# Reordering the first projection and the modulation loads of a one-core transformer block

## The chip, the cores and the metric

The kernel runs on one core of one Trainium2 chip, as one program. The metric is the device time of an execution in microseconds, from three executions of the kernel before. The profile is one further execution, taken by the hardware profiler.

Engines are named as the profile names them: PE (TensorE), PEld (its weight loads), DVE (VectorE), ACT (ScalarE), POOL (GpSimd), SP (SyncE, which issues the DMAs).

## The reference, cut to what matters

Two blocks are computed for 512 positions of 1024 channels. Only the first lines of the first block matter here:

```
mod = silu(c) @ w_ada + b_ada                  # 6 x 1024 numbers, from one vector c
shift1, scale1, gate1, shift2, scale2, gate2 = split(mod)
h = rms_norm(x, norm1_w) * (1 + scale1) + shift1
proj = h @ w_in                                # split into dn_q, dn_k, dn_v, ..., gates
q, k, v = silu(causal_dwconv(dn_q, dn_k, dn_v))
o_a = gated_delta_rule(l2_norm(q), l2_norm(k), v, g, beta)   # recurrence over 8 chunks of 64
o_a = rms_norm(o_a) * silu(dn_z)
...
x = x + gate1 * (mix @ w_o)
h2 = rms_norm(x, norm2_w) * (1 + scale2) + shift2
```

The first third of `mod` (shift1, scale1) is needed before the first projection; the other two thirds (4 x 1024 numbers) only after the first attention halves are done.

## The kernel before, in words

Everything is held transposed: 128 partitions of channels by 512 positions, eight such tiles (k = 0 to 7) for the 1024 channels. Every large product is made of three matmuls (`mm3`, L313): the weight and the activation are each split into a rounded high part (made on ACT, `hi`, L295) and the rest (made on DVE, `lo`, L296), and high x high, high x low and low x high are summed in PSUM (L314, L315, L316). `wload` (L298) fetches a weight tile (512 KB, `raw`) through SP and splits it; one tile is 24 matmuls of 128x512, a "group" below.

**The prologue** (L395 to L481). SP loads the vectors, X in two halves, the constants, then four tiles of w_ada1. PE first multiplies zeros (`zero`), then makes half of the scale row as a matrix-vector product (`adrow`, L417, eight matmuls of one row), which ACT copies and PE turns into a column (`adcol`, L423). ACT squares X tile by tile, DVE sums the squares (`acc`), PE adds them over partitions (`ssx`, L445), ACT makes `rstd` from it (Ln and Exp, which need another activation table than silu). The other modulation numbers of this stage are sums of products on DVE (`on_dve`, L429: one load of 512 KB and one reduction each, `ad`). For every k, DVE multiplies X by rstd (L471), ACT applies scale and shift (L472) and the result is split into H. The first five weight tiles (`FIRST`: misc, 8, 9, 0, 1; `praw`, `phi`, `plo`) are loaded between these steps, and then 120 matmuls run, five groups at a time over k (`mm3`, at the end of the block).

**The stages t = 0 to 5** (L871 on). `merge` interleaves lists of steps by given fractions: projections with their convolution (`proj_steps`; ACT and DVE read PSUM, `cacc` L558, L560), preparation of the recurrence for one pair of heads (`pre_steps`), the recurrence itself (`chain_steps(p)` for pair p = t - 2), gates, and `ada`. `chain_steps` is the chain below: over eight chunks PE makes `pw`, DVE `vn`, PE `ss` and `pc`, DVE the new state S, and so on; after the last `pc`, ACT finishes o and sums its squares (`os`), DVE makes an inverse root of it in a row of small instructions (`rsa`, `rsy`, `rst`, `rsqrt`), multiplies (`o<-o,rsy`, L831), and PE transposes (`tpo`, L835).

**The later modulation** (`ada_steps`, L330). The other 32 columns of `mod` are 64 loads of 256 KB (`adraw`, two buffers) and 64 reductions on DVE with silu(c) held in `cb`. `NADA` gives the stages t = 0 to 5 none, 2, 2, 2, 4 and 6 of the 16 steps, that is 0, 8, 8, 8, 16 and 24 loads.

The order on each engine is set by the framework's scheduler, which starts from the order in which the program is written and moves an instruction ahead of others where its operands and buffers allow it. `tc.keep_in_program_order` takes an instruction out of that. In the kernel before, the load of `cb` and the loads of `adraw` are free, so they are found far ahead of the place where they are written: the first four reductions run at 63 to 72 us.

Of the kernel before, what the change touches and what calls it, by code (L numbers as in the profile page):

```python
# [8 lines left out]
F32 = mybir.dt.float32  # L9
F32R = mybir.dt.float32r  # L10
I32 = mybir.dt.int32
AF = mybir.ActivationFunctionType
ALU = mybir.AluOpType
AX = mybir.AxisListType

P = 128
T = 512
D = 1024
KD = 8
# [193 lines left out]
def _body(ctx, tc, A):  # L213
    nc = tc.nc
# [19 lines left out]
    def C(name, i=0, n=None):  # L234
        o, m = CO[name]
        t = DC[0] if name in DNAMES else CS
        return t[:, o + i:o + (m if n is None else i + n)]
# [5 lines left out]
    eps = C("cst", 0, 1)  # L243
# [26 lines left out]
    def acts(func, **kw):  # L270
        i = nc.scalar.activation(func=func, **kw)
        before.append(i)
        table[0] = None
        return i
# [43 lines left out]
    PSM = [None]  # L318
# [11 lines left out]

    def ada_steps(pl):
        cb = pl.tile([P, D], F32, name="cb")
        nc.sync.dma_start(out=cb, in_=A["crow"].to_broadcast([P, D]))
        acts(func=AF.Silu, out=cb, in_=cb)

        def one(j):
            if j % 4 == 0:
                st["am"] = pl.tile([P, 4, 2], F32, tag="am", name="am", bufs=2)
            for jj in (j, j + 1):
                for q in range(2):  # L340
                    raw = pl.tile([P, T], F32, tag="adraw", name="adraw", bufs=2)
                    qs = slice(q * T, q * T + T)
                    nc.sync.dma_start(out=raw, in_=A["w_adaT"][12 + jj][:, qs])
                    nc.vector.tensor_tensor_reduce(out=raw, in0=raw, in1=cb[:, qs], scale=1.0, scalar=0.0,
                                                   op0=ALU.mult, op1=ALU.add, accum_out=st["am"][:, jj % 4, q:q + 1])
            if j % 4 == 2:
                o = mod[:, 14 + j:18 + j]
                nc.vector.tensor_tensor(out=o, in0=st["am"][:, :, 0], in1=st["am"][:, :, 1], op=ALU.add)
                nc.vector.tensor_tensor(out=o, in0=o, in1=V("b_ada", 14 + j, 4), op=ALU.add)

        st = {}
        return [lambda j=j: one(j) for j in range(0, 32, 2)]
# [30 lines left out]
    FIRST = ("misc", 8, 9, 0, 1)  # L383
    dpx = ExitStack()
    pst = dpx.enter_context(pool("pst", 1, PS))
    ppre = dpx.enter_context(pool("ppre", 1, PS))
    fpx = ExitStack()
    pfirst = fpx.enter_context(pool("pfirst", 3, PS))
    pz = fpx.enter_context(pool("pz", 1, PS))
    PS0 = {}  # L390
# [4 lines left out]
    with pool("w0", 1) as w0:  # L395
        nc.sync.dma_start(out=VS, in_=A["vecs"])
        X0 = w0.tile([P, KD, T], F32, name="X0")
# [11 lines left out]
        def ad_tile():  # L409
            return w0.tile([P, D], F32, tag="ad", name="ad", bufs=15)  # L410

        row_ps = pst.tile([P, T], F32, tag="st", name="adrow")
        for q in range(4):
            raw = ad_tile().rearrange("p (k c) -> p k c", k=2)
# [17 lines left out]
            nc.vector.tensor_tensor_reduce(out=raw, in0=raw, in1=cb, scale=1.0, scalar=0.0,  # L432
                                           op0=ALU.mult, op1=ALU.add, accum_out=am[:, m:m + 1])

        def sadd(out, a, b):
            nc.vector.tensor_tensor(out=out, in0=a, in1=b, op=ALU.add)

        acc = w0.tile([P, T], F32, name="acc0")
        for k in range(KD):
            sq = acc if k == 0 else w0.tile([P, T], F32, tag="sq", name="sq", bufs=2)  # L440
            nc.scalar.activation(out=sq, in_=X0[:, k], func=AF.Square)
            if k:
                sadd(acc, acc, sq)
        ss = ppre.tile([P, T], F32, tag="pre", name="ssx")
        nc.tensor.matmul(ss, C("ones"), acc, start=True, stop=True)  # L445
        rstd = w0.tile([P, T], F32, name="rstd")
        actf(AF.Ln, out=rstd, in_=ss, scale=1.0 / D, bias=eps)
        actf(AF.Exp, out=rstd, in_=rstd, scale=-0.5)

        W0 = {}  # L450

        def first_w(i):
            if i == "misc":
                W0[i] = wload(A["w_misc"], KD, 80, w0)
            else:
                W0[i] = wload(A["w_dn"][i], KD, P, w0)
            PS0[i] = (PSM[0] if i in FIRST[:2] else pfirst).tile([P, T], F32, tag="mm", name="mm")

        sadd(mod[:, 8:12], colp[:, 0:4], V("b_ada", 8, 4))
        nc.vector.scalar_tensor_tensor(out=s1[:, 0:4], in0=mod[:, 8:12], scalar=1.0, in1=V("norm1_w", 0, 4),  # L460
                                       op0=ALU.add, op1=ALU.mult)
        order = {0: 8, 1: 9, 2: "misc", 3: 0, 4: 1}
        for k in range(KD):
            if k >= 4:
                on_dve(4 + k, 8 + k)
                sadd(mod[:, 8 + k:9 + k], am[:, 8 + k:9 + k], V("b_ada", 8 + k))
                nc.vector.scalar_tensor_tensor(out=s1[:, k:k + 1], in0=mod[:, 8 + k:9 + k], scalar=1.0,
                                               in1=V("norm1_w", k), op0=ALU.add, op1=ALU.mult)
            on_dve(k, k)
            sadd(mod[:, k:k + 1], am[:, k:k + 1], V("b_ada", k))  # L470
            nc.vector.tensor_tensor(out=X0[:, k], in0=X0[:, k], in1=rstd, op=ALU.mult)  # L471
            nc.scalar.activation(out=X0[:, k], in_=X0[:, k], func=AF.Identity, scale=s1[:, k:k + 1],  # L472
                                 bias=mod[:, k:k + 1])
            split(X0[:, k], H[0][:, k], H[1][:, k])
            if k < len(FIRST):
                first_w(order[k])
        for k in range(KD):
            for i in FIRST:
                o = PS0[i][:80] if i == "misc" else PS0[i]
# [1292 lines left out]
```

## Time and profile before

| | us |
|---|---|
| three executions | 2159.71, 2162.78, 2163.23 |
| median | 2162.78 |
| the profiled execution | 2166.11 |
| its span, first to last instruction | 2164.3 |
| PE busy in the span | 2130.5 (98%) |
| DVE busy, ACT busy | 1210.5, 898.0 |
| mean granted clock of PE | 0.991 |

The span is the time between the first and the last instruction of the profiled execution; its whole time is 1.8 us longer, and 3.3 us above the median of the three. Rows give a start in us from the start of the span, a duration, the engine, the line, the operation, output<-inputs and how many are taken together; in square brackets stands how long the engine had been idle before, and what ended it. An fp32 matmul of 128x512 that is not split (`adrow`, `ssx`) shows as two entries.

### The profile page before, as it was taken

What the parts mean: (1) busy time and instruction counts of PE and PEld (TensorE: products, weight loads), DVE (VectorE), ACT (ScalarE), POOL (GpSimd) and SP (SyncE); (2) the same over time, 40 slices, a digit from 0 to 9 for tenths busy, and PEclk for the clock granted to TensorE, in tenths of its full rate; (3) what the DMA queues carried; (4) which work ended last, traced back from release to release, by engine and by line L of the source; (5) the groups of instructions that cost most, each with busy time, mean ns of one, the idle gap of its engine ahead of it and who ended that gap; (6) DMA issues with size and microseconds to landing.
All of it is one profiled execution on the core that took longest, in us unless ns stands there. A gap on an engine that the chain in (4) does not pass through costs nothing.

```text
span 2164.3 us, 27485 instructions
## 1 busy us (share of the span) xinstructions
PE 2130.5 (98%) x10616; PEld 1725.6 (80%) x10616; DVE 1210.5 (56%) x2267; ACT 898.0 (41%) x1479; POOL 18.6 (1%) x50
## 2 busy tenths in 40 slices
PE   8999999999999999999999999999999999999997
PEld 5787877788888878888888887887778888888886
DVE  6686767465554554444335898545544454334446
ACT  5645433465553353333224223634443343224333
POOL 0000000000000000000000000000000000000000
PEclk9899999999999999999999999999999999999999
DMA  7443324222224343333333222232222433333332
GB/s 294 136 124 101 97 73 152 62 69 72 67 73 133 103 133 110 105 113 95 92 99 117 80 83 83 74 98 83 87 75 83 147 98 98 96 98 97 93 97 76
DMA packets 88682, 219.84 MB, mean 102 GB/s; under 512 B 23512, under 2 KB 28776, under 8 KB 87912
## 3 DMA queue, kind: packets, MB, share of 16 engines
q1 hardware_dynamic: 88552, 218.10, 32.5%
q8 instruction: 83, 1.36, 0.3%
q14 instruction: 47, 0.39, 0.1%
HBM read 211.50 MB, written 7.08 MB: 101 GB/s over the span
## 4 chain that ended last, share of the span: by engine, by line
PE 89%; DVE 6%; ACT 2%; issue 1%; DMA 1%; SPq 1%; DVEq 0%; ACTq 0%
PE mm L314 24%; PE mm L315 24%; PE mm L316 24%; PE pp L720 2%; DVE yc L1309 1%; DVE lo L296 1%; PE bpo L1637 1%; PE po L1082 1%; PE tps L1246 1%; PE tps L1247 1%; PE tps L1248 1%; PE ssp L602 1%; ACT hi L295 1%; PE pw L793 1%; PE pc L820 1%
## 5 line engine op out<-in xcount | busy, mean ns | idle before, releaser
L295 ACT ACTIVATE hi<-raw 128x1024 fp32r<-128x1024 f32 (+4 forms) x349 | 346.5, 993 | 777.0 <-PE mm L315 676.3
L296 DVE TENSOR_TENSOR lo<-raw,hi 128x1024 fp32r<-128x1024 f32 (+4 forms) x349 | 397.8, 1140 | 438.6 <-ACT hi L295 426.7
L314 PE MATMUL mm<-H,hi 128*128 128x512 f32 x816 | 326.9, 401 | 5.5 <-DVE G L524 4.2
L316 PE MATMUL mm<-H,lo 128*128 128x512 f32 x816 | 325.1, 398 | 0.0
L315 PE MATMUL mm<-H,hi 128*128 128x512 f32 x816 | 324.7, 398 | 0.0
L314 PEld LDWEIGHTS mm<-H,hi 128*128 128x128 f32 x816 | 154.8, 190 | 40.4 <-ACT hi L295 4.6
L316 PEld LDWEIGHTS mm<-H,lo 128*128 128x128 f32 x816 | 154.5, 189 | 32.7 <-issue 3.0
L315 PEld LDWEIGHTS mm<-H,hi 128*128 128x128 f32 x816 | 154.5, 189 | 32.1 <-issue 3.0
L314 PE MATMUL mm<-XN,hi 128*128 128x512 f32 (+1 forms) x456 | 180.1, 395 | 0.0
L315 PE MATMUL mm<-XN,hi 128*128 128x512 f32 (+1 forms) x456 | 179.7, 394 | 0.0
L316 PE MATMUL mm<-XN,lo 128*128 128x512 f32 (+1 forms) x456 | 179.3, 393 | 0.0
L316 PEld LDWEIGHTS mm<-XN,lo 128*128 128x128 f32 (+1 forms) x456 | 85.1, 187 | 19.1 <-issue 1.7
L314 PEld LDWEIGHTS mm<-XN,hi 128*128 128x128 f32 (+1 forms) x456 | 85.1, 187 | 18.9 <-ACT hi L295 0.9
L315 PE MATMUL mm<-HN,hi 128*128 128x512 f32 x256 | 100.0, 391 | 0.0
L314 PE MATMUL mm<-HN,hi 128*128 128x512 f32 x256 | 99.6, 389 | 0.0
L314 PE MATMUL mm<-F,hi 128*128 128x512 f32 x256 | 99.6, 389 | 0.0
L315 PE MATMUL mm<-F,hi 128*128 128x512 f32 x256 | 99.6, 389 | 0.0
L316 PE MATMUL mm<-F,lo 128*128 128x512 f32 x256 | 99.6, 389 | 0.0
L316 PE MATMUL mm<-HN,lo 128*128 128x512 f32 x256 | 99.6, 389 | 0.0
L315 PEld LDWEIGHTS mm<-XN,hi 128*128 128x128 f32 (+1 forms) x456 | 85.0, 186 | 17.8 <-issue 1.4
L1309 DVE SCALAR_TENSOR_TENSOR yc<-cp,cdh,yc 128x512 f32<-128x512 f32 x120 | 89.8, 750 | 2.9
L314 PE MATMUL mm<-FF,hi 128*128 128x512 f32 x176 | 68.5, 389 | 0.0
(676 smaller groups left out, 3909.2 us busy)
## 6 DMA issues: line engine op xcount, KB each, us to landing
raw<-in_w_ff SPq DMA_DIRECT2D x64, 512.0 KB, 3.6
raw<-in_ffn_up SPq DMA_DIRECT2D x44, 512.0 KB, 3.6
adraw<-in_w_adaT SPq DMA_DIRECT2D x64, 256.0 KB, 3.1
raw<-in_w_ga SPq DMA_DIRECT2D x32, 512.0 KB, 3.6
raw<-in_w_dn SPq DMA_DIRECT2D x28, 512.0 KB, 3.7
raw<-in_w_br SPq DMA_DIRECT2D x32, 256.0 KB, 2.6
raw<-in_ffn_down SPq DMA_DIRECT2D x16, 448.0 KB, 3.4
ad<-in_w_adaT SPq DMA_DIRECT2D x12, 512.0 KB, 10.2
```

Source lines behind the costliest of these rows:

```text
L295: nc.scalar.activation(out=hi, in_=src, func=AF.Copy)
L296: nc.vector.tensor_tensor(out=lo, in0=src, in1=hi.bitcast(F32), op=ALU.subtract)
L314: nc.tensor.matmul(ps, wh, xh, start=start, stop=False)
L315: nc.tensor.matmul(ps, wh, xl, start=False, stop=False)
L316: nc.tensor.matmul(ps, wl, xh, start=False, stop=stop)
L602: nc.tensor.matmul(ssp[64 * h:64 * h + 64, kind * 8 + c:kind * 8 + c + 1], sq[:, c], C("ones", 0, 1), start=True, stop=True)
L720: nc.tensor.matmul(pp[:, c4], lh[:, c4], rh[:, c4], start=True, stop=True)
L793: nc.tensor.matmul(pw[64 * h:64 * h + 64], st["wt"][b][:, c4, 64 * h:64 * h + 64], S[:, h], start=True, stop=True)
L820: nc.tensor.matmul(pc[:, 0], ATT[(2 * p + b) % 4][:, c4], vn, start=True, stop=True)
L1082: nc.tensor.matmul(po[:, qs], VT[:, kb, hh], pT[:, kb * P:kb * P + P], start=(kb == 0), stop=(kb == qb))
L1246: nc.tensor.matmul(o_, xh, wh[:, k % 4], start=(k == 0), stop=False)
L1309: i = nc.vector.scalar_tensor_tensor(out=ycs[m], in0=cps[m][:, s:s + T], scalar=cdh[:, m * 31 + s:m * 31 + s + 1], in1=ycs[m], op0=ALU.mul ...
```

## The change

It makes four edits.

- In the prologue the squares, their sum, `ssx`, `rstd` and all eight X*rstd are written ahead of the `adrow` product.
- The first weight tile of the first projection (number 8) is loaded there too, ahead of the four w_ada1 loads. The other four follow in the loop over k, one step earlier than before.
- In `ada_steps` the load of `cb` and its silu move into the first step (j = 0), so that they come in stage t = 1.
- That load and the 64 `adraw` loads are kept in program order.

```
     def ada_steps(pl):
         cb = pl.tile([P, D], F32, name="cb")
-        nc.sync.dma_start(out=cb, in_=A["crow"].to_broadcast([P, D]))
-        acts(func=AF.Silu, out=cb, in_=cb)
 
         def one(j):
+            if j == 0:
+                tc.keep_in_program_order(nc.sync.dma_start(out=cb, in_=A["crow"].to_broadcast([P, D])))
+                acts(func=AF.Silu, out=cb, in_=cb)
...
-                    nc.sync.dma_start(out=raw, in_=A["w_adaT"][12 + jj][:, qs])
+                    tc.keep_in_program_order(nc.sync.dma_start(out=raw, in_=A["w_adaT"][12 + jj][:, qs]))
...
+        ss = ppre.tile([P, T], F32, tag="pre", name="ssx")
+        nc.tensor.matmul(ss, C("ones"), acc, start=True, stop=True)
...
+        for k in range(KD):
+            nc.vector.tensor_tensor(out=X0[:, k], in0=X0[:, k], in1=rstd, op=ALU.mult)
...
+        order = {0: 8, 1: 9, 2: "misc", 3: 0, 4: 1}
+        first_w(order[0])
         row_ps = pst.tile([P, T], F32, tag="st", name="adrow")
...
-            nc.vector.tensor_tensor(out=X0[:, k], in0=X0[:, k], in1=rstd, op=ALU.mult)
...
-            if k < len(FIRST):
-                first_w(order[k])
+            if k < 4:
+                first_w(order[k + 1])
```

Over the whole program the two kernels issue the same matmuls, transfers and DVE instructions; the changed one has one activation table load fewer on ACT. From about 450 us on, all engines have the same order in both. The places that the prediction speaks of follow, as the two kernels issue them.

PE in the prologue, before (`ad` is a w_ada1 tile, `acc0` the sum of squares):

```order
L417 MATMUL adrow_121<-ad_134,csil_119 1x512 [waits DMAHW7_49]
L417 MATMUL adrow_121<-ad_134,csil_119 1x512
L445 MATMUL ssx_172<-acc0_149,CS_58 128x512 [waits DMAHW3_49,DVE_49]
L423 MATMUL adcol_140<-CS_58,adrow0_138 128x1 [waits Activation_49]
L423 MATMUL adcol_140<-CS_58,adrow0_138 128x1 x3
L314 MATMUL mm_209<-H_73,phi_204 128x512 [waits Activation_49]
```

and now:

```order
L406 MATMUL zero_100<-wz_98 128x512 x17
L423 MATMUL ssx_144<-acc0_121,CS_58 128x512 [waits DMAHW3_49,DVE_49]
L446 MATMUL adrow_165<-ad_166,csil_119 1x512 [waits DMAHW5_49,Activation_49]
L446 MATMUL adrow_165<-ad_166,csil_119 1x512
L446 MATMUL adrow_165<-ad_170,csil_119 1x512 [waits DMAHW6_49]
```

The matmul of squares stood behind the eight adrow matmuls and stands ahead of them now.

DVE at the end of pair 1's chain, now (`os` is the sum of squares of o, `lo_3124` the low part of the weight group mm_3128, UK and TK belong to the preparation of pair 2):

```order
L280 TENSOR_SCALAR rsa_2767<-os_2018 128x8 [waits Activation_49]
L345 ISA adraw_2879,am_2878<-adraw_2879,cb_493 128x512 [waits DMAHW6_49]
L345 ISA am_2878 128x1
L695 TENSOR_TENSOR UK_2286<-UK_2286,TK_2516 64x6x10 [waits DVE_49]
L281 TENSOR_SCALAR rsy_2768<-rsa_2767 128x8 [waits DVE_49]
L345 ISA adraw_2882,am_2878<-adraw_2882,cb_493 128x512 [waits DMAHW7_49]
...
L286 TENSOR_TENSOR rst_2769<-rst_2769,rsa_2767 128x8 [waits DVE_49]
L282 TENSOR_SCALAR rsy_2933<-rsy_2933 128x16 [waits DVE_49]
L695 TENSOR_TENSOR UK_2286<-UK_2286,TK_2559 64x4x12 [waits DVE_49]
L287 SCALAR_TENSOR_TENSOR rsy_2768<-rst_2769,rsy_2768 128x8 [waits DVE_49]
L296 TENSOR_TENSOR lo_3124<-raw_3122,hi_3123 128x1024
```

and PE there, now, from the last pc on:

```order
L823 MATMUL pc_2708<-vn_2706,att3_449 128x128 [waits DVE_49]
L314 MATMUL mm_2978<-H_73,hi_2973 128x512
L315 MATMUL mm_2978<-H_73,hi_2973 128x512
L316 MATMUL mm_2978<-H_73,lo_2974 128x512
L314 MATMUL mm_3128<-H_73,hi_3123 128x512 [waits Activation_49]
L315 MATMUL mm_3128<-H_73,hi_3123 128x512
L314 MATMUL mm_3251<-H_73,hi_3246 128x512 [waits DVE_49]
L315 MATMUL mm_3251<-H_73,hi_3246 128x512
L316 MATMUL mm_3128<-H_73,lo_3124 128x512 [waits DVE_49]
```

Before, PE there read:

```order
L820 MATMUL pc_2708<-vn_2706,att3_449 128x128 [waits DVE_49]
L316 MATMUL mm_2978<-H_73,lo_2974 128x512
L314 MATMUL mm_2978<-H_73,hi_2973 128x512
L315 MATMUL mm_2978<-H_73,hi_2973 128x512
L316 MATMUL mm_2978<-H_73,lo_2974 128x512
L314 MATMUL mm_3128<-H_73,hi_3123 128x512 [waits DVE_49]
L315 MATMUL mm_3128<-H_73,hi_3123 128x512
L316 MATMUL mm_3128<-H_73,lo_3124 128x512
```

and went on with mm_3128 to its end and nine matmuls of mm_3251 before tpo; lo_3124 had been made some fifty DVE instructions ahead of rsa. Now PE takes up mm_3251 in between, and the first product with lo_3124 waits for DVE; tpo comes 21 matmuls behind it.

PE at the end of pair 3's chain, now:

```order
L823 MATMUL pc_4067<-vn_4065,att3_449 128x128 [waits DVE_49]
L315 MATMUL mm_4229<-H_73,hi_4224 128x512
L316 MATMUL mm_4229<-H_73,lo_4225 128x512
L314 MATMUL mm_4229<-H_73,hi_4224 128x512
L315 MATMUL mm_4229<-H_73,hi_4224 128x512
L316 MATMUL mm_4229<-H_73,lo_4225 128x512
L838 MATMUL tpo_4091<-CS_58,o_3632 128x128 [waits DVE_49,Activation_49]
L838 MATMUL tpo_4091<-CS_58,o_3632 128x128 x3
L838 MATMUL tpo_4098<-CS_58,o_3632 128x128 [waits DVE_49,PE_49]
L838 MATMUL tpo_4098<-CS_58,o_3632 128x128 x3
L314 MATMUL mm_4320<-H_73,hi_4315 128x512 [waits Activation_49]
```

Before, 40 matmuls of mm_4229 and mm_4320 and one stps stood between this pc and the first tpo. On DVE three adraw reductions and a low part now stand among the small instructions between rsa and `o<-o,rsy`, and none did before; the rope instructions (L925 to L937), which stood among them before, come after tpo.

## Rows read from the trace of the kernel before

**Rows 1.** The page, busy time, share of the span and instructions of each engine.

```profile
PE 2130.5 (98%) x10616; PEld 1725.6 (80%) x10616; DVE 1210.5 (56%) x2267; ACT 898.0 (41%) x1479; POOL 18.6 (1%) x50
```

**Rows 2.** Stretches of the span: microseconds; busy time of each engine with its instructions in brackets; the granted clock of PE as a share of full speed; the share that the DMA engines were busy; GB/s.

```profile
10.00:15.00 5.00, 4.34 (x7) 0.79 (x8) 2.75 (x4) 1.80 (x3) 0.00 (x0) 0.66 1.03 397
25.00:30.00 5.00, 2.82 (x6) 1.90 (x7) 5.00 (x9) 4.30 (x7) 0.00 (x0) 0.52 1.04 414
70.00:75.00 5.00, 0.79 (x4) 0.71 (x4) 4.78 (x10) 4.81 (x8) 0.00 (x0) 0.80 0.54 134
75.00:80.00 5.00, 5.00 (x17) 4.25 (x17) 3.43 (x9) 4.64 (x9) 0.00 (x0) 0.52 0.19 75
85.00:90.00 5.00, 5.00 (x53) 4.40 (x53) 1.51 (x5) 4.58 (x6) 0.00 (x0) 0.67 0.58 210
90.00:95.00 5.00, 5.00 (x27) 3.69 (x26) 0.55 (x2) 0.00 (x0) 0.00 (x0) 0.65 0.00 0
```

**Rows 3.** Timeline of the prologue, PE, DVE and ACT: start, duration, engine, line, operation, output<-inputs, how many together, and idle time before.

```profile
1.43 5.93 PE L405 MATMUL zero<-wz 128*128 128x512 f32 x18 [1.43 <-POOL wz L402]
7.58 5.47 DVE L436 TENSOR_TENSOR acc<-acc,sq 128x512 f32<-128x512 f32 x7 [7.58 <-ACT sq L441]
10.66 8.72 PE L417 MATMUL adrow<-ad,csil 128*1 128x512 f32 x16 [3.30 <-ACT sq L441]
19.31 1.13 PE L445 MATMUL ssx<-acc,CS 128*128 128x512 f32 x2
21.45 0.16 DVE L436 TENSOR_TENSOR mod<-adcol,VS 128x4 f32<-128x4 f32 x1 [2.74 <-PE adcol L423]
21.73 1.22 DVE L296 TENSOR_TENSOR plo<-praw,phi 128x1024 fp32r<-128x1024 f32 x1
22.87 1.22 DVE L432 CUSTOM_DVE_ANT_0 ad<-ad,cb 128x1024 f32<-128x1024 f32 x1
24.01 0.68 DVE L471 TENSOR_TENSOR X<-X,rstd 128x512 f32<-128x512 f32 x1
24.73 1.52 ACT L472 ACTIVATE X<-X,mod,s 128x512 f32<-128x512 f32 x2 [1.61 <-DVE X L471]
26.82 0.79 PE L314 MATMUL mm<-H,phi 128*128 128x512 f32 x1 [5.41 <-ACT H L295]
```

**Rows 4.** Timeline of the stage behind the first projection and of the first row of 128x1 matmuls, PE, DVE and ACT.

```profile
57.81 1.10 PE L511 MATMUL aps<-DC,mab 16*64 16x8 f32 x32
59.72 1.28 ACT L271 ACT_TABLE_LOAD   x1
62.52 1.06 ACT L271 ACTIVATE cb<-cb 128x1024 f32<-128x1024 f32 x1
63.61 0.69 DVE L344 CUSTOM_DVE_ANT_0 adraw<-adraw,cb 128x512 f32<-128x512 f32 x1 [0.89 <-ACT cb L271]
69.62 0.39 PE L316 MATMUL mm<-H,lo 128*128 128x512 f32 x1
73.33 0.74 DVE L560 SCALAR_TENSOR_TENSOR cacc<-mm,VS,cacc 128x509 f32<-128x509 f32 x1
74.22 0.77 PE L314 MATMUL mm<-H,hi 128*128 128x512 f32 x1 [4.21 <-DVE G L524]
79.48 0.57 PE L316 MATMUL mm<-H,lo 128*128 128x512 f32 x1
79.88 0.39 PE L314 MATMUL mm<-H,hi 128*128 128x512 f32 x1
84.06 1.09 PE L602 MATMUL ssp<-CS,dsq 128*64 128x1 f32 x16
```

**Rows 5.** Timeline of the end of pair 1's chain, PE and DVE.

```profile
297.05 0.38 PE L820 MATMUL pc<-vn,att 128*128 128x128 f32 x2
300.60 0.15 DVE L280 TENSOR_SCALAR rsa<-os 128x8 f32<-128x8 f32 x1
301.47 0.67 DVE L344 CUSTOM_DVE_ANT_0 adraw<-adraw,cb 128x512 f32<-128x512 f32 x1
304.57 1.22 DVE L831 TENSOR_TENSOR o<-o,rsy 128x1024 f32<-128x1024 f32 x1
305.95 0.63 PE L835 MATMUL tpo<-CS,o 128*128 128x128 f32 x4
```

**Rows 6.** The instructions of the tile adraw: durations of one in ns, shortest, median and longest; DVE's waits for its loads in us, and how many; us from the issue of a load to its landing.

```profile
L344 DVE CUSTOM_DVE_ANT_0 adraw<-adraw,cb x64: 672/682/694, 63.6 to 368.4; 128x512 f32<-128x512 f32 x64
  DMA adraw<-in_w_adaT: 5.7, 6
DMA to landing us min/median/max: 2.5/3.1/7.2
```

**Rows 7.** Timeline of the end of pair 3's chain, PE and DVE.

```profile
425.68 0.49 PE L820 MATMUL pc<-vn,att 128*128 128x128 f32 x2
427.47 0.17 DVE L280 TENSOR_SCALAR rsa<-os 128x8 f32<-128x8 f32 x1
434.69 1.22 DVE L831 TENSOR_TENSOR o<-o,rsy 128x1024 f32<-128x1024 f32 x1
436.06 0.63 PE L835 MATMUL tpo<-CS,o 128*128 128x128 f32 x4
437.37 0.87 DVE L838 SCALAR_TENSOR_TENSOR OA<-tpo,VS,zs 128x256 f32<-128x256 f32 x2
```

More of the change, by code (lines that the diff above doesn't have):

```diff
@@ L410, in ad_tile, with sadd, first_w @@
             return w0.tile([P, D], F32, tag="ad", name="ad", bufs=15)
+        def sadd(out, a, b):
+            nc.vector.tensor_tensor(out=out, in0=a, in1=b, op=ALU.add)
+        acc = w0.tile([P, T], F32, name="acc0")
+        for k in range(KD):
+            sq = acc if k == 0 else w0.tile([P, T], F32, tag="sq", name="sq", bufs=2)
+            nc.scalar.activation(out=sq, in_=X0[:, k], func=AF.Square)
+            if k:
+                sadd(acc, acc, sq)
+        ss = ppre.tile([P, T], F32, tag="pre", name="ssx")
+        nc.tensor.matmul(ss, C("ones"), acc, start=True, stop=True)
+        rstd = w0.tile([P, T], F32, name="rstd")
+        actf(AF.Ln, out=rstd, in_=ss, scale=1.0 / D, bias=eps)
+        actf(AF.Exp, out=rstd, in_=rstd, scale=-0.5)
+        for k in range(KD):
+            nc.vector.tensor_tensor(out=X0[:, k], in0=X0[:, k], in1=rstd, op=ALU.mult)
+        W0 = {}
+        def first_w(i):
+            if i == "misc":
+                W0[i] = wload(A["w_misc"], KD, 80, w0)
+            else:
+                W0[i] = wload(A["w_dn"][i], KD, P, w0)
+            PS0[i] = (PSM[0] if i in FIRST[:2] else pfirst).tile([P, T], F32, tag="mm", name="mm")
+        order = {0: 8, 1: 9, 2: "misc", 3: 0, 4: 1}
+        first_w(order[0])
         row_ps = pst.tile([P, T], F32, tag="st", name="adrow")
@@ L433, in on_dve @@
                                            op0=ALU.mult, op1=ALU.add, accum_out=am[:, m:m + 1])
[L435 to L457, printed above, removed]
         sadd(mod[:, 8:12], colp[:, 0:4], V("b_ada", 8, 4))
@@ L461, in _body @@
                                        op0=ALU.add, op1=ALU.mult)
-        order = {0: 8, 1: 9, 2: "misc", 3: 0, 4: 1}
         for k in range(KD):
```

## The prediction

> **What bounds the kernel now.** I read the engine lines first: TensorE (PE) is busy 98% of the span [rows 1], so a change pays only where PE stands still or runs slowly, and costs wherever it makes PE stand still. The windows table shows where that is: PE is idle or half-clocked in the first 35 us and at 70 to 80, and half-clocked again, busy, at 85 to 95 [rows 2]. The granted clock falls from 1.00 to 0.52 after an idle stretch and stays there: the 4.21 us of idle that end at 74.22 are followed by matmuls at half speed up to 79.88 (0.57 for the last slow one, at 79.48, 0.39 for the next) [rows 2, 4]. So one long wait costs its own length and about 2.8 us more (half of 5.65). The reader should keep that price: 4.2 of wait costs 7.
>
> Next I read the timeline at the places where the order of instructions differs: the prologue [rows 3], the first stage after it [rows 4], and the ends of two recurrence chains [rows 5, 7]. From about 450 us on both kernels issue the same instructions in the same order.
>
> **The prologue, +2 (0 to +3).** Nothing is added or removed; the matmul of squares (ssx) goes ahead of eight adrow matmuls, X*rstd goes ahead of the modulation reductions on DVE, and one weight load is issued ahead of the four w_ada1 loads on SP. At 414 GB/s [rows 2] a 512 KB load takes 1.27 us, so the w_ada1 loads, crow and the first w_adaT load land 1.27 later and the next three weight tiles 1.27 earlier.
> Now: acc is complete at 13.05 (7.58 + 5.47), PE last worked at 7.36 (1.43 + 5.93) [rows 3]. Before, adrow filled that gap from 10.66; now PE waits until 13.1. That is 5.7 us idle instead of 3.3, and the shorter one already gave 0.66 in the window 10 to 15 [rows 2]. I take half clock for the same 4.2 us as before. ssx: 1.13 at full clock [rows 3], about 1.8 here, to 14.9. An adrow matmul at full clock: (8.72 less 2.1 lost to the clock) / 8 = 0.83 [rows 3]. Eight are 6.6, of which 1.2 is done by 17.3; the rest ends at 22.7 instead of 19.38. From there to mod<-adcol took 2.07 (21.45), so 24.8. DVE then has one reduction (1.22) ahead of s: 26.1. Here the gain comes in: before, X was ready for ACT only at 24.73, 3.3 after mod, because a weight's low part (plo), a reduction and X*rstd stood between [rows 3]; now X waits for s alone. The first main matmul came 2.09 after ACT's X (26.82 - 24.73), so at 28.5 to 29 instead of 26.82. At full clock throughout, the same sum gives 26.8. X*rstd itself costs nothing: 8 x 0.68 = 5.4 us of DVE from about 16 to 21.4, while PE does adrow.
>
> **The stage at 57.8 to 80, -6.5 (-7 to 0).** Before, the crow load, its silu on ACT and four reductions were prefetched into this stage. The change takes out of ACT one table load (1.28) and, for now, the silu (1.06) with the table load that stands between beta and it (1.28), and out of DVE four reductions of 0.76 [rows 4]. They were on the path: PE's third weight group starts at 74.22 when DVE has read the first group's PSUM (last convolution step 73.33, read by 74.07; the profile names the DVE instruction right behind it), 16.3 after aps began. Adding ACT's and DVE's remaining rows in their new order gives 12.1 after aps. PE has two groups of work until 12.2. So the idle of 4.21 goes to about 0.2 (-4.0) and the clock does not fall (-2.8); I take -6.5.
>
> **Clock around the small matmuls, -1 (-3.4 to +2.8).** The windows at 85 to 95 are busy, yet at 0.67 and 0.65: 3.4 us lost [rows 2], after rows of 128x1 matmuls (ssp, 84.06) [rows 4]. The change regroups these; one row of 32 of them is longer, others are shorter.
>
> **The end of pair 1's chain, +7 (0 to +8.3).** The 64 reductions are now loaded in program order, so they move from early, slack places into later ones. After pair 1's last pc, PE now has three matmuls of the running group, two of the next (mm_3128), two of the one after that, and then waits for lo_3124; nothing else is ready. On DVE lo_3124 stands behind rsa, two reductions and about twelve short instructions. Before, lo_3124 had been made some fifty DVE rows earlier, PE ran 37 matmuls straight (8.5 us) and tpo followed o with 0.2 idle [rows 5].
> Sum from the last pc: rsa follows after 1.8 (pair 3, rows 7) to 3.55 (pair 1, rows 5, behind other work); I take 2.3. Two reductions 2 x 0.75, twelve short ones at 0.1 (nine lay in the 0.87 from 300.60 to 301.47), the low part 1.22 (as plo, rows 3): ready at 6.2. PE's own work until then: pc 0.25 and seven matmuls of 0.23, 1.9. Idle 4.3, the same size as the wait at 70, so the same 2.8 for the clock: +7. If rsa takes 3.55 it is +8.3; if DVE reaches lo_3124 before pc, nothing.
>
> **The end of pair 3's chain, +10 (0 to +14).** Stage t=5 now holds 20 reductions in and after this chain. Before, 40 matmuls (9.1 us) stood between the last pc at 425.68 and tpo at 436.06, and covered the normalisation of o, whose last product started at 434.69 [rows 7]. Now five do (1.2 us); the others were spent inside the chain. Without any reduction, rsa at +1.8, eleven short instructions at 0.2 and o*rsy (1.22) make 5.2, so PE idles at least 3.8. With them: two buffers, so each load starts when the reduction two before it is done and lands 3.1 later [rows 6]. The reduction behind the fourth short instruction can start at 2.9, then a lo (1.2), the second ends at 5.6, the third lands at 6.7 and ends at 7.4, and o*rsy ends at 9.0. PE had 1.4 us of work: idle 7.6. Then the clock, 2.8; some of it is hidden, since stps waits for sqa behind two more reductions and four OA products (0.87 a pair, rows 7) until 13.6 anyway: 2.4. Of the rope steps, which filled DVE beside this chain before, some ten us now come after tpo; PE has forty matmuls (9.1) meanwhile, so I cost them at nothing, and mst is what is late next.
> The Trainium skill (DMA: Bandwidth & Descriptors, section Anatomy of one DMA) gives about 2.0 us fixed plus bytes / 436 GB/s, an estimate of 2.6 for these 256 KB. The median here is 3.1, the minimum 2.5 [rows 6]. By the page this term would be about 9 and the time 2174; by the rows it is 10, and I go by them.
>
> **Waits for landings inside the chains, +1 (0 to +4).** Before, DVE waited 5.7 us in six places for these loads [rows 6], nearly all without harm. With two reductions to a chain step of some 4 us, loaded through two buffers at about 3.9 a round (3.1 + 0.75), the short steps wait a little.
>
> **Sum.** 2 - 6.5 - 1 + 7 + 10 + 1 = +12.5 on the profiled execution of 2166.1, which is 3.3 above the median of the three runs. Against the median 2162.8 that is **2175**.
>
> **Rivals.** (1) *Faster, 2158.* DVE has the low part and the normalised o ready in time at both chain ends, and what is left is the removed wait at 70 to 74 with its clock: 2 - 6.5 - 1 + 1 = -4.5. For it: that wait is certain and long, and PE's orders before met their operands almost everywhere (tpo 0.15 after o, rows 5). Against it: the matmuls that covered 8.5 and 9.1 us there are no longer there. It decides if both stalls together stay under 4.5 us. (2) *One stall of the two, 2168.* Pair 1's lo is early after all (+5.5 in all), or pair 3's reductions land early (+2.5). Its lower half is close to no change. (3) *The gain at 70 does not come, 2182.* The prologue delivers its five PSUM groups later, or G or the convolution is late for another reason; the change then only delays. Against it: all removed rows are on ACT and DVE ahead of the 73.33 step. (4) *They cancel, 2163:* each stall idles PE about 2 us, and the clock holds: 2 x 2 against -4.5. Nothing in my rows shows what a wait of 2 us does to the clock.
>
> **Chances.** Forecast 0.44, (1) 0.20, (2) 0.18, (3) 0.08, (4) 0.10. About 0.2% (4.3 us) is what a measurement of this kernel can tell from no change. Slower takes the forecast, (3) and most of (2): 0.66; same takes (4) and the lower part of (2): 0.14; faster is (1): 0.20. The likeliest case's own range is 2168 to 2184 (one chain stall at its low end, or both near their high ends). The range for 8 in 10 reaches down to rival (1), 2157, and up to 2186, where (3) and the high ends of both stalls lie.
>
> **What would show it.** Right: ssx ahead of adrow, the first main matmul at 28 to 29; no PE idle of over 1 us at about 70 and a clock of 1.00 behind it; then a PE wait of about 4 us for lo ahead of pair 1's tpo and one of 7 us for o ahead of pair 3's, each followed by a stretch at about 0.5. Wrong: if PE's list of waits holds no entry of over 2 us for DVE between 250 and 450 us, the two big terms are gone and rival (1) holds; if adraw lands much later than 3.1 us, the chain term is too small; if the wait at 70 is still there, (3).

## The result, and the profile after

| | before | after |
|---|---|---|
| median, us (4 executions each, on one chip) | 2162.65 | **2192.51** |
| profiled execution, its span | 2166.1, 2164.3 | 2191.1, 2189.3 |

The changed kernel is slower: the measured ratio is 1.0146 (interval 1.0134 to 1.0158), and the medians differ by +29.9 us, where +12.5 was forecast. Between the two profiled executions the difference is 25.0. The other 4.9 come from the two profiles themselves: that of before lies 3.5 above its median, that of after 1.4 below. The profiled execution of one later run, the one with nothing in t=5, took 2268 us at a mean granted clock of 0.885; it is left out of that run's time, and none of its rows is used.

All of it has arisen by about 500 us: from the second `mst<-msq` (L1027 before, at 476.73; L1030 after, at 501.87) to the end both take 1687.5. A split of that first part tells what kind of time it is. Windows of 2.5 us give *idle* (length less PE busy) and *clock* (busy times one less granted clock). The 1170 main matmuls take 0.2267 each, their spacing in the dense runs; *rest* is what remains: the small matmuls, which are the same in all kernels, and waits too short or too hidden to show as idle. Before: idle 17.4, clock 13.6, rest 180.5. After: idle 33.3, clock 17.1, rest 186.2. Such sums are good to about 0.3.

The page's first part of after, which answers [rows 1]; PE is as busy as ever:

```profile
PE 2139.9 (98%) x10616; PEld 1730.0 (79%) x10616; DVE 1216.0 (56%) x2267; ACT 897.5 (41%) x1478; POOL 18.5 (1%) x50
```

Windows of after, columns as in [rows 2], first the stage behind the prologue and the first row of small matmuls, then the ends of pairs 1 and 3:

```profile
70.00:75.00 5.00, 4.73 (x22) 3.60 (x20) 4.24 (x9) 4.44 (x8) 0.00 (x0) 1.00 0.38 105
75.00:80.00 5.00, 5.00 (x26) 3.83 (x24) 2.98 (x7) 4.81 (x9) 0.00 (x0) 1.00 0.00 0
85.00:90.00 5.00, 5.00 (x37) 3.79 (x36) 1.35 (x2) 2.52 (x3) 0.00 (x0) 0.67 0.01 3
90.00:95.00 5.00, 5.00 (x19) 4.00 (x19) 4.08 (x9) 0.18 (x1) 0.00 (x0) 0.64 0.21 48
300.00:305.00 5.00, 3.08 (x7) 2.48 (x8) 5.00 (x23) 0.03 (x1) 0.00 (x0) 0.68 0.72 206
440.00:445.00 5.00, 0.00 (x0) 0.00 (x0) 4.58 (x16) 1.17 (x3) 0.00 (x0) 0.67 0.44 134
445.00:450.00 5.00, 2.20 (x9) 1.86 (x10) 2.56 (x9) 1.15 (x2) 0.00 (x0) 0.50 0.53 159
450.00:455.00 5.00, 5.00 (x17) 3.64 (x17) 4.78 (x10) 0.00 (x0) 0.00 (x0) 0.80 0.20 49
465.00:470.00 5.00, 3.50 (x15) 3.28 (x16) 5.00 (x9) 3.95 (x11) 0.00 (x0) 0.56 0.00 0
470.00:475.00 5.00, 5.00 (x18) 4.04 (x17) 4.02 (x8) 2.81 (x5) 0.00 (x0) 0.76 0.00 0
```

The reader should see the forecast gain at 70 to 80 (clock 1.00, where [rows 2] has 0.80 and 0.52), the same loss as before at 85 to 95, and what came new: a window at 300 with PE busy 3.08, and 440 to 445 without one PE instruction, DVE busy 4.58 of those 5 us, with two stretches of reduced clock behind it (0.50 and 0.56 in their slowest windows).

PE of after, the prologue, the ends of pairs 1 and 3 and the rope, the rows that answer [rows 3, 4, 5, 7]:

```profile
13.02 2.08 PE L423 MATMUL ssx<-acc,CS 128*128 128x512 f32 x2 [5.66 <-DVE acc L414]
29.11 0.72 PE L314 MATMUL mm<-H,phi 128*80 128x512 f32 x1 [3.64 <-ACT H L295]
60.37 1.10 PE L514 MATMUL aps<-DC,mab 16*64 16x8 f32 x32
72.84 0.47 PE L314 MATMUL mm<-H,hi 128*128 128x512 f32 x1 [0.27 <-ACT t L265]
...
296.09 0.38 PE L823 MATMUL pc<-vn,att 128*128 128x128 f32 x2
297.86 0.50 PE L314 MATMUL mm<-H,hi 128*128 128x512 f32 x1 [0.69 <-ACT GT L271]
301.92 0.80 PE L316 MATMUL mm<-H,lo 128*128 128x512 f32 x1 [2.87 <-DVE lo L296]
...
437.13 0.38 PE L823 MATMUL pc<-vn,att 128*128 128x128 f32 x2
445.46 1.09 PE L838 MATMUL tpo<-CS,o 128*128 128x128 f32 x4 [6.79 <-DVE o L834]
448.89 1.09 PE L838 MATMUL tpo<-CS,o 128*128 128x128 f32 x4 [2.34 <-DVE OA L841]
462.39 0.39 PE L316 MATMUL mm<-H,lo 128*128 128x512 f32 x1
465.14 1.46 PE L1016 MATMUL mst<-CS,msq 128*128 128x1 f32 x8 [2.36 <-DVE msq L1013]
467.96 0.79 PE L314 MATMUL mm<-OAs,hi 128*128 128x512 f32 x1 [1.36 <-ACT OAs L295]
```

DVE of after at the same two ends:

```profile
298.12 0.17 DVE L280 TENSOR_SCALAR rsa<-os 128x8 f32<-128x8 f32 x1
299.02 0.68 DVE L345 CUSTOM_DVE_ANT_0 adraw<-adraw,cb 128x512 f32<-128x512 f32 x1
300.66 1.21 DVE L296 TENSOR_TENSOR lo<-raw,hi 128x1024 fp32r<-128x1024 f32 x1
...
438.77 0.17 DVE L280 TENSOR_SCALAR rsa<-os 128x8 f32<-128x8 f32 x1 [0.47 <-ACT junk L829]
439.47 0.68 DVE L345 CUSTOM_DVE_ANT_0 adraw<-adraw,cb 128x512 f32<-128x512 f32 x1
440.16 1.22 DVE L296 TENSOR_TENSOR lo<-raw,hi 128x1024 fp32r<-128x1024 f32 x1
441.30 0.68 DVE L345 CUSTOM_DVE_ANT_0 adraw<-adraw,cb 128x512 f32<-128x512 f32 x1
443.08 0.69 DVE L345 CUSTOM_DVE_ANT_0 adraw<-adraw,cb 128x512 f32<-128x512 f32 x1 [0.21 <-DMA adraw<-in_w_adaT]
444.09 1.22 DVE L834 TENSOR_TENSOR o<-o,rsy 128x1024 f32<-128x1024 f32 x1
447.18 0.69 DVE L345 CUSTOM_DVE_ANT_0 adraw<-adraw,cb 128x512 f32<-128x512 f32 x1 [1.25 <-DMA adraw<-in_w_adaT]
447.80 0.48 DVE L841 SCALAR_TENSOR_TENSOR OA<-tpo,VS,zs 128x256 f32<-128x256 f32 x1
450.81 0.68 DVE L365 TENSOR_TENSOR sqa<-sq 128x512 f32<-128x512 f32 x1
451.41 0.42 DVE L929 CAST tn<-pi 128x512 f32<-128x512 int32 x1
464.41 0.68 DVE L1013 TENSOR_TENSOR msq<-msq,qsq 64x512 f32<-64x512 f32 x1
```

Before, the rope (L925 to L937) began at 417.2, far ahead of the pair's last pc (the row gives shortest, median and longest in ns, and first and last start):

```profile
L926 DVE CAST tn<-pi x1: 419/419/419, 417.2 to 417.2; 128x512 f32<-128x512 int32 x1
```

PE's rows of the prologue and of the stage are close to the forecast: ssx waits 5.66 (5.7) and takes 2.08 at reduced clock (1.8), the first main matmul comes at 29.11 (28.5 to 29), and 0.27 is left of the 4.21 at 70. Behind pair 3's last pc the normalisation of o is interrupted by three reductions and a low part, as the sum had it. Then comes the part to which the sum gave no time: a reduction that waits 1.25 for its landing stands ahead of the OA products that the second tpo waits for, and the rope begins at 451.41 and brings msq only at 464.41, when PE has run out of other work (its last matmul ahead of mst starts at 462.39).

The loads of the tile adraw themselves did not become slower (it answers [rows 6]):

```profile
  DMA adraw<-in_w_adaT: 6.6, 10
...
DMA to landing us min/median/max: 2.5/3.0/4.5
```

### The profile page after: what moved, and what is told of

Same layout as the page of the kernel before. It is cut to its first block, busy times and chain, and to the rows that moved or that the text cites. A ratio compares the mean times of both kernels' runs of the same rounds, so it can differ in the third digit from the quotient of the medians.

```text
span 2189.3 us, 27509 instructions
## 1 busy us (share of the span) xinstructions
PE 2139.9 (98%) x10616; PEld 1730.0 (79%) x10616; DVE 1216.0 (56%) x2267; ACT 897.5 (41%) x1478; POOL 18.5 (1%) x50
## 3 DMA queue, kind: packets, MB, share of 16 engines
q8 instruction: 83, 1.36, 0.3%
## 4 chain that ended last, share of the span: by engine, by line
PE 88%; DVE 6%; ACT 2%; issue 1%; DMA 1%; SPq 1%; DVEq 0%; ACTq 0%
PE mm L314 24%; PE mm L315 24%; PE mm L316 24%; PE pp L723 2%; DVE lo L296 1%; DVE yc L1312 1%; PE bpo L1640 1%; PE po L1085 1%; PE tps L1249 1%; PE tps L1250 1%; PE tps L1251 1%; PE ssp L605 1%; PE ss L813 1%; PE pw L796 1%; PE pc L823 1%
## 5 line engine op out<-in xcount | busy, mean ns | idle before, releaser
L314 PE MATMUL mm<-XN,hi 128*128 128x512 f32 (+1 forms) x456 | 180.2, 395 | 0.0
```

The costliest lines, as they stand in the source:

```text
L314: nc.tensor.matmul(ps, wh, xh, start=start, stop=False)
```

## The experiments

Each ran beside executions of the kernel before (medians 2161.1 to 2162.1). "Gaps" are PE instructions between last pc and tpo for the four pairs; idle, clock and rest are as above, in the run's own profile.

**The two halves of the change.** The prologue alone (`ada_steps` as before):

> The change's prologue alone; crow and the modulation loads of the later stages as before. Theory P (the loss sits in the later loads): only what the trace of the change shows up to aps, 60.37 against 57.81, so +2.6: 2164 to 2167, with the PE wait of 4.2 us at 70 to 74 still there. Rival Q (the prologue's delay shifts the stages against their loads and costs again later): +8 or more, above 2170.

2162.45, ratio 1.0006 (0.9994 to 1.0018): no difference clear of noise. Rival Q's 8 or more is excluded; P's +2.6 is not, since the interval reaches from 1 us less to 4 more. Two windows of its profile, where PE has the order of the kernel before:

```profile
85.00:90.00 5.00, 5.00 (x62) 4.20 (x60) 0.69 (x1) 3.49 (x5) 0.00 (x0) 1.00 0.36 115
90.00:95.00 5.00, 5.00 (x21) 3.78 (x22) 4.57 (x13) 1.37 (x2) 0.00 (x0) 1.00 0.28 66
```

The clock was full there; in [rows 2] it was 0.67 and 0.65. So the 3.4 us at this clump can go without any change of order at the clump itself, with another prologue ahead of it. The idle time of PE that ends at 73.93 was 2.61, not 4.21: the later start is swallowed by that wait, since the matmul behind it started at 74.22 in the kernel before.

The modulation alone (prologue as before, `ada_steps` as in the change):

> The later modulation loads kept in program order, with crow and silu in stage 1; prologue as before. Theory P: the change without its prologue, so 27 us above before (29.9 less 2.6): 2187 to 2192, with the waits for lo ahead of pair 1's tpo (2.9 us), for o ahead of pair 3's tpo (6.8) and for msq (2.4) unchanged. Rival Q: below 2184.

2191.86, ratio 1.0141 (1.0124 to 1.0158): the whole loss, as P has it. It has after's five waits between 290 and 470 (2.88 for lo, 6.57 for o, 1.58 for OA, 2.36 for msq, 1.48 for OAs).

**Only cb in program order.**

```
-                    tc.keep_in_program_order(nc.sync.dma_start(out=raw, ...[:, qs]))
+                    nc.sync.dma_start(out=raw, ...[:, qs])
```

> Only the load of crow is kept in program order (with silu in stage 1); the 64 loads behind it are free again, prologue as before. In its order the matmuls between last pc and tpo are 56, 40, 45 and 39 for the four pairs, as many as before (60, 37, 40, 40). Theory P (the loss is loads bound to late places, where nothing covers the chain ends): the wait at 70 goes with its slow clock, no wait over 2 us at the chain ends: 6 below before, 2153 to 2159. Rival R (reductions taken out of the first stage cost about as much wherever they come later): 2163 to 2175.

2178.02, ratio 1.0070 (1.0047 to 1.0092): a miss for theory P, and above R's range too. The ends of pairs 1 to 3 have no wait of over 0.7 ahead of tpo and rest is 181.6, but clock is 22.2, of which 13.6 at 200 to 215 and 285 to 300, where ssp rows stand close together; and behind pair 3's tpo PE waits 4.47 for ACT (qrr, at 452.79), with 3.2 more lost to the clock.

**Nothing in t=5** (modulation part, its loads moved to the stages ahead):

```
-    NADA = (0, 2, 2, 2, 4, 6)
+    NADA = (0, 2, 4, 4, 6, 0)
```

> As e2, all loads in program order, but the steps are spread 0, 2, 4, 4, 6, 0 over the stages t = 0 to 5, none in t = 5. Theory P: the waits at and behind pair 3's end (about 17 us in the trace of the change) go; pair 1's end still has few matmuls (29), so its wait may stay: 2162 to 2172. Rival S (program order itself is the price, since SP then holds weight loads behind waiting adraw loads): 2180 or more.

2172.75, ratio 1.0050 (1.0035 to 1.0065), just above P's range: 19.1 of the loss come back, though all 64 loads are still kept in order, so S fails. Only its time is used.

**Another queue.** The loads kept in order, but issued by POOL:

```
-tc.keep_in_program_order(nc.sync.dma_start(out=raw, ...
+tc.keep_in_program_order(nc.gpsimd.dma_start(out=raw, ...
```

> The modulation part alone (prologue as before), all 64 loads still in program order, but issued by POOL's queue and not by SP's, so that the weight loads and the load of pi stand behind none of them. The number of PE instructions between a chain's last pc and its tpo is then 50, 77, 42 and 42 for the four pairs (before 76, 37, 40, 41; changed kernel 47, 28, 40, 5). Theory P (the loss comes from the cover that is gone at the chain ends, and it goes because the loads hold up SP's queue): no PE wait of over 2 us between 290 and 470 us, the wait of 4.2 us at 70 gone with its clock: 2153 to 2160. Theory Q (64 reductions late in the program cost by themselves, inside the chains on DVE, wherever their loads are issued): 2175 to 2190. Theory R (the clock falls at runs of small matmuls, whose places move with any change of order): 2160 to 2178, with no wait of over 2 us but more than 17 us of slow clock.

2174.88, ratio 1.0064 (1.0049 to 1.0078). The cover at the ends is back (gaps 50, 77, 42, 42) and 17 us come back with it (2191.86 to 2174.88); the other 13 stay, so P's 2153 to 2160 fails. Clock is 11.8, so it is not R's either: idle is 21.6 and rest 185.7. Q is nearest, whose range begins at 2175. The list of what DVE waited for has

```profile
DVE adraw L345 <- DMA adraw<-in_w_adaT: 19.5, 16, 2.3
```

19.5 us in 16 waits, where it was 5.7 in 6 [rows 6]. How much of it PE had to wait for in turn is not shown.

The whole change with that queue:

> The changed kernel whole, with its prologue, but the 64 loads on POOL's queue. Order from the first projection on as with the old prologue and POOL's queue. Theory P: the later prologue costs 2 to 3 us here, since no wait at 70 is left to absorb it: 2 to 3 above the run with the old prologue, 2155 to 2163. Theory S (the prologue's lateness is absorbed elsewhere too): within 1 us of that run. Theory Q and R: as for that run, 2160 to 2190.

2173.51, ratio 1.0063 (1.0048 to 1.0078), 1.4 less than with the old prologue: nearer S, though with intervals of some 3 us either way P's 2 to 3 more are not excluded.

**Four loads.** Only cb and the first four loads kept (`if jj < 2:`):

> The modulation part alone, but only the load of cb and the first four of the 64 loads are kept in program order; the other 60 are free, as before. The first four reductions leave the stage at 60 to 75, and PE instructions between last pc and tpo are 37, 37, 41 and 38. Theory P: 2153 to 2160 (the wait at 70 gone, nothing lost at the chain ends). Theory R: as with only the load of cb kept, 2165 to 2178, without long waits, through slow clock at runs of small matmuls. Theory Q: as P, since the reductions stay early.

2173.67, ratio 1.0059 (1.0047 to 1.0072): R, though with one longer wait, 2.55 at pair 0's tpo. Rest is 181.3 and idle 18.3, but clock 20.1, half of it in one place. Windows of this run:

```profile
285.00:290.00 5.00, 5.00 (x29) 3.50 (x27) 2.83 (x10) 2.67 (x9) 0.00 (x0) 0.58 0.00 0
290.00:295.00 5.00, 5.00 (x23) 3.49 (x23) 0.76 (x3) 0.00 (x0) 0.00 (x0) 0.50 0.01 3
295.00:300.00 5.00, 5.00 (x31) 3.92 (x27) 1.55 (x7) 0.00 (x0) 0.00 (x0) 0.50 0.00 0
300.00:305.00 5.00, 5.00 (x16) 2.28 (x15) 2.17 (x9) 0.77 (x3) 0.00 (x0) 0.50 0.00 0
```

PE has no idle from 285 to 305 and runs at half clock. A row of 32 ssp came at 282.93, rows of 16 at 289.05 and 295.05, and from 285 to 305 PE has 17 main matmuls, the two rows of 16 and 40 other small ones; full clock returns at about 307, in the dense run behind pair 1's last pc.

**The last 24 loads** of the kernel before kept, the rest free (`if jj >= 20:`):

> The kernel before, with only the 24 loads of stage t=5 kept in program order (cb and the other 40 free). PE instructions between last pc and tpo: 76, 24, 39 and 44. The wait of 4.2 us at 70 stays. Theory P (the cost of t=5 in the changed kernel is the loss of its cover, 41 to 5, and with it the late rope): cover stays, so 2160 to 2167. Theory Q (24 reductions beside pair 3's chain cost by their own DVE time and landings, whatever the cover): the time of the term, 12 to 18 more than before, 2174 to 2181.

2165.10, ratio 1.0017 (1.0007 to 1.0026): P. Kept order in t=5 costs 3.3 where its cover stays (gap 44).

**t=5 later.** The changed kernel with

```
-(0, 0.5, ad)
+(0 if t < 5 else 0.85, 0.5 if t < 5 else 1, ad)
```

> The changed kernel with one number changed: the 24 reductions of stage t=5 are written behind 85% of the stage and not over its first half. The order of PE and DVE is that of the changed kernel up to stage t=5; at the end of pair 3's chain 19 PE instructions now stand between the last pc and the first tpo (5 in the changed kernel), one reduction stands between rsa and o (four and a low part in it), and the rope instructions still come behind the last reductions, after tpo. It parts the two halves of the term at pair 3: theory T (the uncovered normalisation of o, 6.8 of wait with half clock behind it and 2.3 at the second tpo): 6 to 10 of it come back, 2182 to 2187, with a tpo wait of 1 to 3 and the waits behind the rope (msq 2.4, OAs 1.4, second clock fall 2.8) still there. Theory U (the late rope is the cost): 2189 to 2194. Theory V (lost cover is all of the 17): 2174 to 2178.

2186.65, ratio 1.0114 (1.0093 to 1.0134): T's time, by a partly different sum. PE of this run, and the last reduction on DVE:

```profile
441.65 0.63 PE L838 MATMUL tpo<-CS,o 128*128 128x128 f32 x4 [1.49 <-ACT ckv L945]
451.16 2.08 PE L369 MATMUL stps<-sqa,CS 128*128 128x512 f32 x2 [4.94 <-DVE sqa L365]
465.30 1.05 PE L1016 MATMUL mst<-CS,msq 128*128 128x1 f32 x8 [1.57 <-DVE msq L1013]
...
448.76 0.69 DVE L345 CUSTOM_DVE_ANT_0 adraw<-adraw,cb 128x512 f32<-128x512 f32 x1 [2.10 <-DMA adraw<-in_w_adaT]
```

Of the 6.79 ahead of tpo 1.49 are left, and 4.94 stand ahead of stps instead: DVE still has its reductions to do ahead of sqa and the rope, and the last of them waits 2.10 for its load. The wait for OAs and the second fall of the clock, which T expected to stay, are gone (1.00 from 465 to 475). A wait that is moved away from tpo comes back further down.

**silu(c) kept from the prologue**, for the later reductions too:

```
-        cb = w0.tile([P, D], F32, name="cb0")
+        cb = CB[0] = dcp.tile([P, D], F32, name="cb0")
...
-        cb = pl.tile([P, D], F32, name="cb")
-        nc.sync.dma_start(out=cb, in_=A["crow"].to_broadcast([P, D]))
-        acts(func=AF.Silu, out=cb, in_=cb)
+        cb = CB[0]
```

> The kernel before, but silu(c) in all partitions, which the prologue makes anyway, is kept and used by the later reductions: the second load of 512 KB, the second silu and the activation table loads around it are gone; the 64 loads stay free and the first four reductions stay in the stage at 60 to 75. PE instructions between last pc and tpo: 62, 78, 38, 41. Theory P (ACT's silu and table loads, 3.6 us, are on the path to the wait at 70): that wait falls from 4.2 to under 1.5 and the clock holds, 2154 to 2159. Theory Q (the four reductions on DVE are what holds PE there): wait of 3 to 4 stays, 2160 to 2164. Theory R (any new order of the later stages moves the runs of small matmuls and with them the clock): 2165 to 2178, wherever the wait at 70 stands.

2162.85, ratio 1.0006 (0.9996 to 1.0016): in Q's range, without Q's wait of 3 to 4. The wait at 70 falls only to 2.71 and is followed by half clock up to 80, and 5.1 us more are lost to the clock at 205 to 217. With X*rstd early as well:

> As the run with silu(c) reused, and X*rstd moved ahead of the modulation reductions in the prologue, while the adrow products stay ahead of ssx and the weight loads where they were. Behind the first projection the order is that of the other run. Theory P: the prologue's first main matmul comes 0.5 to 2 us earlier than 26.8, and the time is 0 to 2 below the other run. Theory S (ACT waits for s, not for X): no difference, within 1 us.

2162.71, ratio 1.0004 (0.9995 to 1.0013): S. The first main matmul did not come earlier either (26.10, and 25.16 without the move).

**No later modulation at all**, `mod`'s 32 columns being b_ada alone:

> The kernel before without its later modulation: the load of cb, its silu, the 64 loads and the 64 reductions are left out, and the 32 columns are b_ada alone. It bounds what any place for them can bring. The scheduler spends more matmuls inside the chains: 60, 36, 23 and 23 PE instructions between last pc and tpo. Theory P (PE-bound, the reductions cost only where they lengthen a wait of PE): 2150 to 2158. Theory Q (reductions cost inside the chains wherever they stand, 0.3 us each in hidden waits): 2135 to 2148. Theory R (clock at runs of small matmuls decides): 2155 to 2172 with over 12 us of slow clock.

2157.02, ratio 0.9978 (0.9969 to 0.9986), clock 6.9, rest 180.2: P. Leaving the 64 loads and reductions out altogether brings 4.7 by the medians; in the profiles the clock alone is 6.7 less. Another place for them could bring more only by a better order of everything else.

**The 40 and the 24 apart**, in the changed kernel: without t=5's 24 (`if j < 20:` around the loop), then without the first 40 (`if j >= 20:`, with the load of cb in t=5). The columns of `mod` that are left out are b_ada alone.

> The changed kernel without the 24 loads and reductions of stage t=5 (their columns of mod are b_ada alone; left out of the computation). The places of the other 40, the prologue and the ends of pairs 0 and 1 (47 and 28 PE instructions between last pc and tpo) are those of the changed kernel; at pair 3's end 41 stand there and not 5. Theory T (the term at pair 3 was mis-sized: 17 to 19, not 10): 2172 to 2177, with the lo wait of 2.9 and the hidden waits in the chains of pairs 0 to 2 (5 to 6 over before) unchanged. Theory U (the term was right at 10 and the rest was lost all through the chains): 2180 to 2185.

2172.64, ratio 1.0049 (1.0033 to 1.0065): T. The wait for lo ahead of pair 1's tpo (2.9) and the rest (185.6) are as in after; the second `mst<-msq` comes at 483.96 and not 501.87. So t=5's 24 are worth 17.9 in the profile and 19.9 in the median, with no wait ahead of tpo:

```profile
443.26 0.63 PE L842 MATMUL tpo<-CS,o 128*128 128x128 f32 x4
```

> The changed kernel without the 40 loads and reductions of stages t=1 to 4 (left out of the computation); cb and the 24 of stage t=5 come in program order in t=5. PE instructions between last pc and tpo: 60, 36, 29, 37. Theory T (t=5 is dear only because earlier kept loads leave DVE behind there, so that the normalisation of o loses its cover): 2157 to 2165, near the kernel without any later modulation. Theory U (24 reductions and a rope behind them cost 15 or more whatever stands ahead): 2172 to 2180.

2163.13, ratio 1.0007 (0.9997 to 1.0017), rest 181.3: T. The same 24 with nothing ahead of them cost little.

The last three and the changed kernel make a square: neither 2157.0, the 24 alone 2163.1, the 40 alone 2172.6, both 2192.5. The 24 cost 6.1 without the 40 and 19.9 with them. (The first corner has the old prologue, which made no difference clear of noise.) Between pair 3's last pc and tpo stand 23, 37, 41 and 5 PE instructions in the four: only with both is the cover gone. So the 13.8 that the two cost beyond their sum go with the lost cover; whether the work that DVE is late with would cost as much under full cover is not separated.

## Why the prediction was wrong

The direction, the cause (loads in program order put DVE behind at the chains' ends) and the places were right; the size was not, because two of its terms were far too small. By the prediction's own terms, in the profiles:

| term | forecast | measured |
|---|---|---|
| prologue | +2 | +2.6 at aps |
| stage at 57.8 to 80 | -6.5 | -6.7 |
| clock around small matmuls | -1 | -1.7 |
| end of pair 1's chain | +7 | +5.0 |
| end of pair 3's chain | +10 | **+17.6** |
| waits inside the chains | +1 | **+8.2** |
| sum | +12.5 | +25.0 |

**Pair 3: the failed step is "so I cost them at nothing, and mst is what is late next".** The first wait and its clock came out nearly as worked: 6.79 + 2.1 = 8.9 against 7.6 + 2.4. The other 8.7 are what stood behind it: 2.34 at the second tpo, 2.36 at mst, 1.36 at OAs, and a second fall of the clock at 465 (2.8), less 0.2 that stood there before. The sum had listed the two reductions, four OA products and sqa that keep DVE until 13.6 after the last pc (measured 14.4), but used them only to take 0.4 off the clock, and it set some ten us of rope against 9.1 of matmuls. Measured, PE's cover was longer, 48 matmuls and stps from 449.63 to 462.78; but the rope began only at 451.41, 6.0 behind the first tpo, and took 13.7 to the end of msq, in which DVE also made a weight's low part and ckv and waited 2.7 for ACT. The run with t=5 later shows that this is the work DVE is late with and not tpo's place alone: with tpo's wait down to 1.49, stps waited 4.94. The run without the 24 gives back 17.9 in the profile, the size of the whole term. How much of it is the reductions' own time and how much the landing of loads through two buffers (1.25 of waiting here, 2.10 in the run with t=5 later) stays open; no run has more buffers.

**Waits inside the chains: +1 was too small.** Rest rose by 5.7, and idle by some 2.5, in waits of 0.2 to 1.8, the longest for zs and tpo at the ends of pairs 0 and 2. Rest is 185.6 to 187.5 in the six profiles in which the first 40 loads are kept, whatever queue issues them and with or without t=5's 24, and 180.2 to 181.8 in the others. So this part belongs to those 40 where they are kept in order. My reasoning from landings (3.9 a round against a chain step of 4) would have let them wait a little; that the short steps wait behind the 0.75 of a reduction is the likely cause, inferred from the order and not shown place by place.

**Pair 1: +5.0.** rsa came 2.03 after pc and lo was ready 5.8 after it (forecast 2.3 and 6.2). PE's idle fell into two pieces, 0.69 and 2.87, and the clock cost 1.4, not 2.8.

**Stage at 70: right in size, and of little use.** Idle 0.27, clock 1.00. Yet no run with all of the later modulation kept this gain in its time. With cb alone or four loads kept, the clock took more than it elsewhere (22.2 and 20.1, before 13.6); with all 64 kept, idle and rest did. And the wait of 4.2 was a place where delays vanished, as the run with the prologue alone shows.

**Prologue: in the profiles, not seen in the times.** aps comes 2.6 later in the profile (55.5 to 57.8 in eight profiles with the old prologue, 59.1 to 60.4 in six with the new), but three pairs of runs with the old and the new prologue differ by 0.3, 0.6 and -1.4 in their medians, each good to a few us. In the first pair the wait at 70 takes the delay up (73.93 against 74.22 behind it); whether it is taken up in the other two, where that wait is 1.56 with the old prologue and 0.27 with the new, stays open. Inside the sum, the eight adrow matmuls took 8.72 as before, not 7.8: I had taken 2.1 off for the clock, where the window 10 to 15 of [rows 2] gives 1.5.

**The offset.** The median is 4.9 further away than the profiles are. I took 3.3 off the sum's end as if the changed kernel's executions would lie below its profile too; they lie 1.4 above. The clock alone makes differences of this kind: up to 310 us the profile of after loses 12.2 to it, and those of the runs without t=5's 24 and with t=5 later, in which PE has the same order up to there, 13.8 and 15.0. That the 4.9 come from it is not shown.

Rival (1) fell with the first waits; (3) fell with the windows at 70. (2) asked that one of the two stalls stay away and (4) that each be about 2 us; both came, with 3.6 of idle at pair 1 and 12.9 at pair 3.

The Trainium skill (DMA: Bandwidth & Descriptors, section Anatomy of one DMA) gives its fit, an estimate of 2.6 for such a load, for transfers issued by GpSimd, and I had used it for SP's. The median was 3.0 on SP's queue after the change and 3.1 on POOL's in the run with that queue, so the page's figure is too low for the median on either; the shortest took 2.5 and 2.7. The difference would have moved the term by one, away from the result.

## What to carry to other kernels

When a stall is found on a queue of work, follow that engine on past the first instruction that is waited for: cost everything that now stands behind it, up to the point where the engine has caught up, since a wait taken away at one consumer returns at the next. Cost a late placement together with what is late ahead of it; 24 reductions cost 6 alone and 20 behind 40 others that were late too. And before expecting a gain from moving hidden work, time the kernel without it: here that floor was 4.7 us away.

## What the runs showed of the hardware

The granted clock fell to 0.50, half of full speed, while the profile shows PE without a pause: 10.2 us were lost at 285 to 307 in the run with four kept loads, where 17 main matmuls stood among 72 small ones, and the clock rose again in the next dense run. That the small matmuls are the cause is not tested by a run of its own.

The same order of instructions does not always get the same clock. The changed kernel and the run with t=5 later have the same order on PE from the first instruction to 410 us; a window of the first and then of the second:

```profile
125.00:127.50 2.50, 2.50 (x7) 1.91 (x7) 2.50 (x8) 0.63 (x1) 0.00 (x0) 0.50 0.05 14
125.00:127.50 2.50, 2.50 (x16) 2.08 (x15) 1.76 (x7) 1.27 (x3) 0.00 (x0) 1.00 0.37 138
```

From 122 to 130 that is 1.7 us lost in the first and none in the second; at 85 to 100 and at 300 to 310 the second loses about as much more. The kernel before and the run with its last 24 loads kept agree at 85 to 95 (0.67 and 0.65, 0.64 and 0.67), while the prologue alone, with the same order there, has 1.00 and 1.00. So both a change of order and what runs ahead of it move such losses by some us either way, and a single profile does not give their price.
